# Raw blocks of the column-split W2 in tiles of 1024 columns, in a pool that the attention half shares

## The chip, the cores and the metric

The kernel runs on one core of a Trainium2 chip. The metric is the device time of one execution in microseconds (us). Of the kernel before there are three runs: 1780.76, 1771.97 and 1772.99 us, median 1772.99. A profiled execution was taken beside them. The core has TensorE (PE, with its weight loads as PEld), VectorE (DVE), ScalarE (ACT), GpSimd (POOL) and SyncE (SP), and 16 DMA engines.

## The reference

Two layers over 512 tokens of 1024 channels, in float32. Each layer:

```python
u = rms_norm(h, attn_norm[l])
proj = u @ w_in[l]                 # three mixers' q, k, v and the gates
a = differential_attention(...)    # 4 heads
r = bidirectional_retention(...)   # 4 heads
c = grouped_query_attention(...)   # 8 query heads
projected = einsum('bsnw,nwd->bsnd', [a, r, c], w_branch[l])
merged = sum(sigmoid(gates) * projected)
h = h + merged @ w_out[l]
m = square(relu(rms_norm(h, mlp_norm[l]) @ w_mlp_in[l]))   # 1024 -> 4096
h = h + m @ w_mlp_out[l]                                   # 4096 -> 1024 (W2)
```

## The kernel before

Every float32 operand of a matmul is held as two parts, hi and lo: ScalarE copies the operand to hi (a cast), VectorE subtracts hi from it to get lo, and TensorE adds three products (hi·hi, hi·lo, lo·hi). Weights come from memory in blocks of 128x1024 (512 KB) and are cut in this way just before use; `prefetch` does so two steps ahead.

A layer has two halves. In the attention half (`mix`) the projections and gates run woven with the heads (`ret_head`, `diff_head`, `gqa_head`). Each head ends in a pair of tiles hi and lo (`rTh`/`rTl`, `aTh`/`aTl`, `cTh`/`cTl`), which `proj_unit` multiplies by the branch weights, first those of the retention (merge 1), then the differential attention (merge 0), then the grouped attention (merge 2). In the MLP half, W1 runs in pairs of column blocks (`pair`, seven products of 128x256 matmuls each, PSUM tiles `x12`, `x674` and `x53`; each product is copied out by ScalarE to `pu` or `c0`). A pair takes two `stage` loads of 512 KB; the pool `stage` has two buffers. W2 is in four groups of 1024 rows. Groups 0 to 2 (`WIDE_GROUPS`) multiply by seven products of a two-by-two block scheme (`wide_product`), whose left operands are sums of the blocks A11, A12, A22 and A21 of W2. `cut_wide` loads the raw blocks, adds them in place (S1, S2, S4, S3) and cuts the sums; each raw block is held as two tiles of 128x512 out of the pool `g`, each loaded, added and cut by itself. The results of the seven products go to `sums` in memory: written by SyncE for group 0, added by a GpSimd DMA for groups 1 and 2. `gather` reads them back in tiles of 128x512 (`wp`), combines them on VectorE, turns them with TensorE and adds them to `h`, while group 3 runs as plain products.

Nearly all tiles of 128x512, of both halves, come from `g`, which has 51 buffers.

The order of the instructions is not that of the code: all operations are recorded and a planner (`order`) sets the order of each engine ahead of time. It steps through planned time; when an engine is free, it takes the first waiting operation in the recorded order whose inputs are ready and whose tiles have room in their pool (`fits`, where a tile may take a buffer only if those recorded earlier keep theirs). Its prices are `price`, `HOPS` and, for a load of SyncE, bytes / 360 ns and 2000 ns to land. What stands on an engine's list then runs in that order, so an instruction that waits holds back all that stands behind it. Every recorded matmul has line L455 in the profile and nearly every other instruction L461, so rows are told apart by tiles.

```python
            raw[x, k] = [self.g(x) for _ in range(2)]
            for i, t in enumerate(raw[x, k]):
                self.nc.sync.dma_start(out=t, in_=self.a["w"][at][:, i * 512:(i + 1) * 512])
```

Of the kernel before, what the change touches and what calls it, by code (L numbers as in the profile page):

```python
# [170 lines left out]
BUFS_G = 51  # L171
# [300 lines left out]
class Core:  # L472
    def __init__(self, ctx, tc, a):
# [13 lines left out]
        self.p_g = pool("g", BUFS_G)  # L487
        self.p_small = pool("small", 12)
# [26 lines left out]
    def g(self, name, dt=F32):  # L515
        return self.p_g.tile([128, 512], dt, tag="g", name=name)

# [69 lines left out]
    def cut_wide(self, q, op, k):  # L587
# [4 lines left out]
        def load(x):  # L592
            at = q + (int(x[1]) - 1) * 4 + (int(x[2]) - 1) * 2 + k
            raw[x, k] = [self.g(x) for _ in range(2)]
            for i, t in enumerate(raw[x, k]):
                self.nc.sync.dma_start(out=t, in_=self.a["w"][at][:, i * 512:(i + 1) * 512])

        def add(x, y):
            for t, o in zip(raw[x, k], raw[y, k]):
                self.nc.vector.tensor_tensor(out=t, in0=t, in1=o, op=ALU.add)  # L600
# [6 lines left out]
        hi, lo = self.parts(self.p_w, 1024)  # L607
        for i, t in enumerate(raw[x, k]):
            c = slice(i * 512, i * 512 + 512)
            self.nc.scalar.copy(out=hi[:, c], in_=t)  # L610
            self.nc.vector.tensor_tensor(out=lo[:, c], in0=t, in1=hi[:, c], op=ALU.subtract)
        return hi, lo
# [379 lines left out]
    def ret_head(self, h, st):  # L992
# [39 lines left out]
        hi, lo = self.g("rTh", F32R), self.g("rTl", F32R)  # L1032
# [62 lines left out]
    def diff_head(self, h, st):  # L1095
# [53 lines left out]
        hi, lo = self.g("aTh", F32R), self.g("aTl", F32R)  # L1149
# [9 lines left out]
    def gqa_head(self, j, kv, st):  # L1159
# [45 lines left out]
        if kv == 1:  # L1205
            hi, lo = self.g("cTh", F32R), self.g("cTl", F32R)
# [192 lines left out]
    def mlp(self, l, mT, h, mid, load, ready):  # L1399
# [14 lines left out]
        for what, g, i in mlp_order():  # L1414
# [14 lines left out]
            if g in WIDE_GROUPS:  # L1429
                if i == 0:  # L1430
                    rights = self.rights(m)
                    nxt = next(rights)
# [20 lines left out]
    def rights(self, m):  # L1453
# [5 lines left out]
        for n in WIDE_PRODUCTS:  # L1459
# [10 lines left out]
            for i in range(2):  # L1470
                hi, lo = self.g("xh", F32R), self.g("xl", F32R)
# [32 lines left out]
    def gather(self, h, mid, load, rp):  # L1504
# [3 lines left out]
        def back(n, s):  # L1508
            x = self.g("wp")
            nc.sync.dma_start(out=x, in_=self.sums[n, s])  # L1510
# [3 lines left out]
        u2, c = [None, None], [[None] * 4, [None] * 4]  # L1514
        for s in range(2):
            p1, p2, p6, p5, p3 = (back(n, s) for n in (1, 2, 6, 5, 3))
            tt(p2, p1, p2)
            tt(p6, p6, p1, ALU.subtract)
            tt(p5, p5, p6)
            tt(p3, p3, p5, ALU.subtract)  # L1520
            c[0][s], c[0][2 + s], u2[s] = p2, p3, (p6, p5)
        for half in range(2):
            if half:
                for s in range(2):
# [181 lines left out]
```

## Time and profile before

| what | value |
|---|---|
| runs | 1780.76, 1771.97, 1772.99 us; median 1772.99 us |
| profiled execution, its time | 1772.2 us |
| its span, first to last instruction | 1770.4 us |
| PE busy | 1744.6 us, 99% of the span |
| DVE busy | 1484.3 us, 84% |
| ACT busy | 1139.0 us, 64% |
| granted TensorE clock | 1.00 |
| loads of `stage` | 235, 512.0 KB each |
| loads of raw W2 blocks (`A`) | 96, 256.0 KB each |

How to read it: busy time of PE is modelled and matmuls overlap in it, so 99% does not say that TensorE never waits; what it waits for is seen in the waits of its weight loads (PEld). The list of waits names for each engine who waited for whom, in all and the longest. The timeline lists one engine's instructions with the idle time before each. Idle time of an engine that is not waited for costs nothing.

### The profile page before, as it was taken

Reading aid. Unit: us, or ns where it says so; the run is one execution under the profiler, and the core shown is the slowest. Engines: PE = TensorE matmul, PEld = TensorE weight load, DVE = VectorE, ACT = ScalarE, POOL = GpSimd, SP = SyncE. Lnnn points to the kernel's source line nnn. Section 1 sums busy time; section 2 is a strip of 40 time slices with the busy share of each in tenths; the row PEclk is TensorE's granted clock in tenths of the full one; section 3 lists DMA queues with packets and bytes.
Section 4 is the critical chain, followed back from the end, with each engine's and each line's share of the span. In section 5 each row is a group of like instructions: output and inputs, shape, how many; then the busy total and the mean of one; then the engine's idle time right before and its main releaser. Section 6 shows DMA issues by size and latency. Waiting matters only on the chain.

```text
span 1770.4 us, 27228 instructions
## 1 busy us (share of the span) xinstructions
PE 1744.6 (99%) x10136; PEld 1525.3 (86%) x10136; DVE 1484.3 (84%) x2438; ACT 1139.0 (64%) x2064; POOL 339.9 (19%) x350
## 2 busy tenths in 40 slices
PE   8999999999999999999999999999999999999999
PEld 6887888889988989988888778888899899989887
DVE  7866887899978999999866667978999789998994
ACT  5544666785556877777535456768855568777771
POOL 2334463001110001111013235700012100011110
PEclk9999999999999999999999999999999999999999
DMA  6311212112355354747622122111124542646482
GB/s 205 106 61 48 86 66 72 48 48 73 115 183 179 96 178 103 219 96 225 206 93 71 48 76 68 60 60 60 36 97 133 160 172 92 211 99 182 96 249 84
DMA packets 76741, 201.95 MB, mean 114 GB/s; under 512 B 8896, under 2 KB 9408, under 8 KB 76608
## 3 DMA queue, kind: packets, MB, share of 16 engines
q1 hardware_dynamic: 68544, 185.53, 32.0%
q0 software_dynamic: 8064, 14.68, 5.6%
q8 instruction: 79, 1.29, 0.3%
q14 instruction: 54, 0.44, 0.1%
HBM read 169.77 MB, written 30.41 MB: 113 GB/s over the span
## 4 chain that ended last, share of the span: by engine, by line
PE 73%; DVE 11%; DMA 6%; ACT 5%; issue 3%; POOL 2%; SPq 0%; ACTq 0%; DVEq 0%; POOLq 0%
PE x L455 19%; PE wide L455 7%; PE proj L455 6%; PE gate L455 6%; DMA stage<-in_w 6%; PE w L455 5%; PE wo L455 5%; PE c L455 4%; DVE w_lo L461 4%; PE wtr L457 2%; PE rg L455 2%; PE gsc L455 2%; PE gav L455 2%; PE dsc L455 2%; PE rq L455 1%
## 5 line engine op out<-in xcount | busy, mean ns | idle before, releaser
L461 ACT CAST w_hi<-stage 128x1024 fp32r<-128x1024 f32 (+1 forms) x235 | 226.8, 968 | 169.0 <-DMA stage<-in_w 95.4
L461 DVE TENSOR_TENSOR w_lo<-stage,w_hi 128x1024 fp32r<-128x1024 f32 (+1 forms) x235 | 282.0, 1202 | 35.1 <-ACT w_hi L461 31.9
L455 PE MATMUL x<-u,w_hi 128*128 128x256 f32 x1472 | 276.1, 283 | 0.0
L455 PEld LDWEIGHTS x<-u,w_hi 128*128 128x128 f32 x1472 | 233.5, 192 | 2.5
L455 PE MATMUL x<-u,w_lo 128*128 128x256 f32 x736 | 208.3, 283 | 0.0
L461 POOL DMA_DIRECT2D sums<-wp x56 | 49.1, 876 | 560.1 <-ACT xh L461 475.2
L455 PEld LDWEIGHTS x<-u,w_lo 128*128 128x128 f32 x736 | 141.1, 192 | 0.0
L455 PE MATMUL wide<-w_lo,xh 128*128 128x512 f32 x336 | 130.9, 390 | 0.0
L455 PE MATMUL wide<-w_hi,xl 128*128 128x512 f32 x336 | 130.8, 389 | 0.0
L455 PE MATMUL wide<-w_hi,xh 128*128 128x512 f32 x336 | 129.7, 390 | 0.0
L461 DVE TENSOR_TENSOR w_lo<-A,w_hi 128x512 fp32r<-128x512 f32 x168 | 112.3, 684 | 10.3 <-ACT w_hi L461 9.5
L455 PE MATMUL x<-t23h,w_hi 128*128 128x256 f32 x368 | 105.2, 287 | 3.3 <-ACT c L461 3.0
L461 ACT CAST w_hi<-A 128x512 fp32r<-128x512 f32 x168 | 102.2, 621 | 8.2 <-ACT w_hi L461 2.7
L455 PE MATMUL gate<-u,w_hi 128*128 128x512 f32 x320 | 106.4, 399 | 0.0
L461 ACT ACTIVATE c<-c 128x512 f32<-128x512 f32 x156 | 94.0, 628 | 19.0 <-DVE c L461 17.3
L455 PE MATMUL x<-t23h,w_lo 128*128 128x256 f32 x368 | 104.3, 283 | 0.3 <-DVE w_lo L461 0.2
L455 PE MATMUL x<-t23l,w_hi 128*128 128x256 f32 x368 | 104.1, 283 | 0.0
L455 PE MATMUL c<-w_hi,u 128*128 128x512 f32 x256 | 86.1, 394 | 0.0
L455 PEld LDWEIGHTS x<-t23h,w_hi 128*128 128x128 f32 x368 | 70.3, 191 | 5.9 <-ACT c L461 5.3
L461 POOL TENSOR_TENSOR gth<-gth,c 128x512 f32<-128x512 f32 x28 | 40.8, 1465 | 178.1 <-DVE c L461 178.0
L455 PEld LDWEIGHTS wide<-w_hi,xl 128*128 128x128 f32 x336 | 63.1, 188 | 13.1
L455 PEld LDWEIGHTS wide<-w_lo,xh 128*128 128x128 f32 x336 | 63.1, 188 | 12.5
(299 smaller groups left out, 5208.9 us busy)
## 6 DMA issues: line engine op xcount, KB each, us to landing
stage<-in_w SPq DMA_DIRECT2D x235, 512.0 KB, 3.6
A<-in_w SPq DMA_DIRECT2D x96, 256.0 KB, 4.6
sums<-wp POOLq DMA_DIRECT2D x56, 256.0 KB, 6.0
sums<-wp SPq DMA_DIRECT2D x28, 256.0 KB, 2.8
wp<-sums SPq DMA_DIRECT2D x28, 256.0 KB, 4.7
h<-in_x SPq DMA_DIRECT2D x16, 256.0 KB, 4.4
mid<-h SPq DMA_DIRECT2D x16, 256.0 KB, 2.1
h<-mid SPq DMA_DIRECT2D x16, 256.0 KB, 6.3
```

Of the source, the lines that this page charges most:

```text
L455: self.nc.tensor.matmul(k.pop("out"), **k)
L457: self.nc.tensor.transpose(k["out"], k["in_"], k["identity"])
L461: getattr(getattr(self.nc, o.engine), o.name)(**k)
```

## The change

Two pools take the place of one. `g` goes from 51 to 36 buffers of 128x512, and a new pool `b` has 8 buffers of 128x1024 (`big`), 52 buffers' worth of space together. In `b` lie

- the raw blocks of W2: one load of 512 KB for two of 256 KB, one addition of 128x1024 for two of 128x512, one cast and one subtraction for two of each (`part`);
- the hi and lo parts of `rT`, of `aT` and of the last two heads' pairs of `cT`, as the two halves of one tile (`big_parts`);
- the two last operands of the last wide group (`xb`, products 3 and 7);
- the tiles of `gather` (`wpb`): still two loads of 256 KB each, but one addition for both halves.

Count by engine: VectorE has 2292 instructions where it had 2438, ScalarE's casts and copies fall by 84, SyncE issues 428 DMAs for 476, TensorE and GpSimd have as many as before.

```diff
-BUFS_G = 51
+BUFS_G = 36
+BUFS_B = 8
...
+        self.p_b = pool("b", BUFS_B)
...
+    def big(self, name, dt=F32):
+        return self.p_b.tile([128, 1024], dt, tag="b", name=name)
+    def big_parts(self, name):
+        t = self.big(name, F32R)
+        return t[:, 0:512], t[:, 512:1024]
...
         def load(x):
             at = q + (int(x[1]) - 1) * 4 + (int(x[2]) - 1) * 2 + k
-            raw[x, k] = [self.g(x) for _ in range(2)]
-            for i, t in enumerate(raw[x, k]):
-                self.nc.sync.dma_start(out=t, in_=self.a["w"][at][:, i * 512:(i + 1) * 512])
+            raw[x, k] = self.big(x)
+            self.nc.sync.dma_start(out=raw[x, k], in_=self.a["w"][at])
         def add(x, y):
-            for t, o in zip(raw[x, k], raw[y, k]):
-                self.nc.vector.tensor_tensor(out=t, in0=t, in1=o, op=ALU.add)
+            self.nc.vector.tensor_tensor(out=raw[x, k], in0=raw[x, k], in1=raw[y, k], op=ALU.add)
...
-        hi, lo = self.parts(self.p_w, 1024)
-        for i, t in enumerate(raw[x, k]):
-            c = slice(i * 512, i * 512 + 512)
-            self.nc.scalar.copy(out=hi[:, c], in_=t)
-            self.nc.vector.tensor_tensor(out=lo[:, c], in0=t, in1=hi[:, c], op=ALU.subtract)
-        return hi, lo
+        return self.part(self.p_w, 1024, raw[x, k])
...
-        hi, lo = self.g("rTh", F32R), self.g("rTl", F32R)
+        hi, lo = self.big_parts("rT")
...
-        hi, lo = self.g("aTh", F32R), self.g("aTl", F32R)
+        hi, lo = self.big_parts("aT")
...
-            hi, lo = self.g("cTh", F32R), self.g("cTl", F32R)
+            hi, lo = self.big_parts("cTb") if j >= 2 else (self.g("cTh", F32R), self.g("cTl", F32R))
...
-                hi, lo = self.g("xh", F32R), self.g("xl", F32R)
+                hi, lo = self.big_parts("xb") if last and n in (3, 7) else (self.g("xh", F32R), self.g("xl", F32R))
...
-        def back(n, s):
-            x = self.g("wp")
-            nc.sync.dma_start(out=x, in_=self.sums[n, s])
+        def back(n):
+            x = self.big("wpb")
+            for s in range(2):
+                nc.sync.dma_start(out=x[:, s * 512:(s + 1) * 512], in_=self.sums[n, s])
             return x
...
-        for s in range(2):
-            p1, p2, p6, p5, p3 = (back(n, s) for n in (1, 2, 6, 5, 3))
-            tt(p2, p1, p2)
-            tt(p6, p6, p1, ALU.subtract)
-            tt(p5, p5, p6)
-            tt(p3, p3, p5, ALU.subtract)
-            c[0][s], c[0][2 + s], u2[s] = p2, p3, (p6, p5)
+        p1, p2, p6, p5, p3 = (back(n) for n in (1, 2, 6, 5, 3))
+        tt(p2, p1, p2)
+        tt(p6, p6, p1, ALU.subtract)
+        tt(p5, p5, p6)
+        tt(p3, p3, p5, ALU.subtract)
+        c = [both(p2, p3), both(p6, p5)]
```

The planner lays the whole program out anew. Up to the first gates and grouped-attention heads that lie side by side (about 350 us into each layer in the profile) the order on TensorE, VectorE, ScalarE and GpSimd is the same as before; in the merge it differs by some places, and in the MLP half TensorE's order is again nearly the same. Three places follow.

ScalarE in the first layer's attention, where a differential head's exponential `dE1` is written (`dwh` are turned softmax weights, `w_hi` a cut weight block; in brackets what each waits for, numbers tell tiles apart). Before:

```order
L461 CAST dwh_2406<-wtr_2349 128x512 [waits PE_49]
L461 ACTIVATE dE1_2413,dss_2376<-dsc_2367,mx_2392 128x512 [waits DVE_49]
L461 CAST w_hi_2423<-stage_2150 128x1024 [waits DMAHW4_49,PE_49]
L461 CAST w_hi_2438<-stage_2179 128x1024 [waits DMAHW5_49,PE_49]
L461 ACTIVATE dE1_2413<-dE1_2413,drc_2433 128x512 [waits DVE_49,Activation_49]
```

Now:

```order
L463 CAST dwh_2403<-wtr_2346 128x512 [waits PE_49]
L463 ACTIVATE dE1_2410,dss_2373<-dsc_2364,mx_2389 128x512 [waits DVE_49,Pool_49]
L463 CAST w_hi_2420<-stage_2148 128x1024 [waits DMAHW4_49,PE_49]
L463 CAST w_hi_2435<-stage_2177 128x1024 [waits DMAHW5_49,PE_49]
L463 ACTIVATE dE1_2410<-dE1_2410,drc_2430 128x512 [waits DVE_49,Activation_49]
```

The order is the same; the exponential `dE1` of the second row now waits for GpSimd too, since its buffer of `g` was one that a GpSimd instruction used.

ScalarE in the second layer, in the second wide group, where a pair of W1 is cut (`stage`, `sa`) while products are copied out (`c`, `pu`) and raw W2 blocks (`A`) are cut. Before:

```order
L461 CAST xh<-t_17281 128x512
L461 COPY c_17371<-x_17338 128x256
L461 CAST w_hi<-stage 128x512
L461 CAST w_hi<-A_16950 128x512
L461 COPY pu<-x_17342 128x256
L461 COPY c_17371<-x_17338 128x256
L461 CAST w_hi<-A_16852 128x512
L461 CAST xh<-c_16404 128x256
L461 CAST w_hi<-stage 128x1024
```

Now:

```order
L463 COPY c_18014<-x_17987 128x256
L463 COPY pu<-x_18007 128x256
L463 CAST w_hi<-stage 128x512
L463 COPY c_18014<-x_17987 128x256
L463 CAST w_hi<-A_17473 128x1024
L463 CAST xh<-t_17866 128x512
L463 CAST w_hi<-A_17493 128x1024
L463 CAST w_hi<-stage 128x1024
L463 COPY c_18014<-x_17968 128x256
```

Between the cast of the first `stage` block and the next copy to `c` there were a cast of `A` and a copy to `pu`; now that copy stands right behind the cast, the copy to `pu` ahead of it, and the blocks of W2 are cut whole and later.

SyncE in the second layer, from the last loads of the third wide group to the reads of `gather` (`stage` are weight blocks of 512 KB, `A` raw W2 blocks, `wp` and `wpb` the sums read back). Before:

```order
L461 DMA A_17847<-in_w 128x512
L461 DMA A_17855<-in_w 128x512
L461 DMA stage<-in_w 128x1024 x4
L461 DMA A_18185<-in_w 128x512
L461 DMA A_18194<-in_w 128x512
L461 DMA A_18217<-in_w 128x512
L461 DMA A_18229<-in_w 128x512
L461 DMA stage<-in_w 128x1024 x4
L461 DMA wp<-sums_101 128x512
L461 DMA wp<-sums_103 128x512
L461 DMA wp<-sums_107 128x512
```

Now:

```order
L463 DMA A_17493<-in_w 128x1024
L463 DMA A_17507<-in_w 128x1024
L463 DMA A_17528<-in_w 128x1024
L463 DMA stage<-in_w 128x1024 x8
L463 DMA wpb<-sums_104 128x512
L463 DMA wpb<-sums_106 128x512
L463 DMA wpb<-sums_105 128x512
L463 DMA wpb<-sums_110 128x512
L463 DMA wpb<-sums_107 128x512
```

The four late loads of `A` no longer stand between the loads of `stage`, and all eight raw blocks of the group stand ahead of eight loads of `stage`.

## Rows read from the trace of the kernel before

**Rows 1.** The page: its first line, part 1 (busy time of each engine, share of the span, instructions), one line of part 2 (the granted clock in 40 slices, tenths), and one of part 4 (the chain that ended last, by engine).

```profile
span 1770.4 us, 27228 instructions
...
PE 1744.6 (99%) x10136; PEld 1525.3 (86%) x10136; DVE 1484.3 (84%) x2438; ACT 1139.0 (64%) x2064; POOL 339.9 (19%) x350
...
PEclk9999999999999999999999999999999999999999
...
PE 73%; DVE 11%; DMA 6%; ACT 5%; issue 3%; POOL 2%; SPq 0%; ACTq 0%; DVEq 0%; POOLq 0%
```

**Rows 2.** The waits of TensorE's weight loads over the whole run (who waited for whom: us in total, times, longest): seven of the 23 rows, the first and the last among them.

```profile
PEld x L455 <- ACT c L461: 9.6, 17, 1.3
PEld rv L455 <- ACT w_hi L461: 7.1, 1, 7.1
PEld dsc L455 <- ACT dkh L461: 4.0, 6, 0.9
...
PEld qtr L457 <- POOL qk L461: 3.6, 4, 1.3
PEld rav L455 <- DVE sdl L461: 2.1, 1, 2.1
PEld gsc L455 <- ACT gE L461: 1.9, 4, 0.7
...
PEld rav L455 <- ACT sdh L461: 0.2, 1, 0.2
```

**Rows 3.** The same view for the stretch of the first layer's column-split products, 590 to 870 us.

```profile
PEld x L455 <- ACT c L461: 2.6, 5, 1.1
PEld x L455 <- DVE w_lo L461: 0.3, 1, 0.3
```

**Rows 4.** The same view from 1460 us to the end, the second layer's.

```profile
PEld x L455 <- ACT c L461: 5.8, 7, 1.3
...
PEld x L455 <- DVE w_lo L461: 0.4, 1, 0.4
```

**Rows 5.** The same view for 400 to 590 us: the merge of the first layer and the products behind it.

```profile
PEld x L455 <- ACT c L461: 0.6, 3, 0.3
```

**Rows 6.** ScalarE's instructions in order of time, 1568 to 1577 us (start us, us, engine, line, operation, out<-in; in brackets the idle time before it and what ended it).

```profile
1569.92 0.39 ACT L461 COPY c<-x 128x256 f32<-128x256 f32 x1
1573.06 0.62 ACT L461 CAST w_hi<-stage 128x512 fp32r<-128x512 f32 x1 [2.75 <-DMA stage<-in_w]
1573.58 0.61 ACT L461 CAST w_hi<-A 128x512 fp32r<-128x512 f32 x1
1574.10 0.36 ACT L461 COPY pu<-x 128x256 f32<-128x256 f32 x1
1574.37 0.37 ACT L461 COPY c<-x 128x256 f32<-128x256 f32 x1
```

**Rows 7.** TensorE's, in the same microseconds (the gap in brackets is the idle time of the modelled matmul).

```profile
1573.47 0.28 PE L455 MATMUL x<-u,w_lo 128*128 128x256 f32 x1
1574.79 0.39 PE L455 MATMUL x<-t4h,w_hi 128*128 128x256 f32 x1 [1.04 <-ACT c L461]
```

**Rows 8.** The DMA issues of SyncE ahead of them, 1560 to 1577 us.

```profile
1565.24 1.23 SPq L461 DMA_DIRECT2D stage<-in_w  x2
```

**Rows 9.** The view of the tile `stage`, 1440 to 1710 us: time from issue to landing (min, median, max), and then the same view for 100 to 300 us.

```profile
DMA to landing us min/median/max: 3.3/5.4/7.8
...
DMA to landing us min/median/max: 3.4/3.5/4.5
```

**Rows 10.** The waits of ScalarE, 1460 us to the end.

```profile
ACT w_hi L461 <- DMA stage<-in_w: 25.2, 12, 3.6
```

**Rows 11.** Groups by line, engine, operation and shape, 1460 us to the end (busy us, mean ns of one, idle time before them).

```profile
L461 DVE TENSOR_TENSOR w_lo<-A,w_hi 128x512 fp32r<-128x512 f32 x84 | 56.2, 684 | 6.2 <-ACT w_hi L461 5.8
L461 ACT CAST w_hi<-A 128x512 fp32r<-128x512 f32 x84 | 51.1, 621 | 3.8 <-ACT w_hi L461 1.8 <-PE wide L455 1.0 <-DVE A L461 0.8
...
L461 DVE TENSOR_TENSOR A<-A,A 128x512 f32<-128x512 f32 x48 | 31.7, 683 | 0.0
...
L461 DVE TENSOR_TENSOR w_lo<-sb,w_hi 128x1024 fp32r<-128x1024 f32 x13 | 15.8, 1219 | 0.4 <-ACT w_hi L461 0.4
...
L461 ACT CAST w_hi<-sb 128x1024 fp32r<-128x1024 f32 x13 | 13.7, 1054 | 0.8 <-DVE sb L461 0.3
...
L461 DVE TENSOR_TENSOR wp<-wp 128x512 f32<-128x512 f32 x14 | 9.2, 683 | 0.0
```

**Rows 12.** Busy time by stretch: the column-split products of the first and the second layer.

```profile
core 0: us, PE busy (x) PEld busy (x) DVE busy (x) ACT busy (x) POOL busy (x), PEclk, DMA share, GB/s
590.00:870.00 280.00, 278.33 (x1748) 251.67 (x1747) 263.23 (x460) 209.91 (x400) 24.61 (x28) 1.00 0.58 160
1460.00:1720.00 260.00, 255.44 (x1646) 232.51 (x1645) 238.91 (x428) 197.05 (x389) 24.46 (x28) 1.00 0.56 152
```

**Rows 13.** The DMA issues of the stretch 1440 to 1710 us (count, KB each, median us to landing).

```profile
stage<-in_w SPq DMA_DIRECT2D x28, 512.0 KB, 5.4
A<-in_w SPq DMA_DIRECT2D x36, 256.0 KB, 4.6
sums<-wp POOLq DMA_DIRECT2D x28, 256.0 KB, 6.4
```

**Rows 14.** In the first layer's attention: the GpSimd instructions from 232 us, then the ScalarE instructions from 241 us, then the same two for 264 and 274 us.

```profile
233.23 1.29 POOL L461 TENSOR_TENSOR gqx<-gqx,axy 128x512 f32<-128x512 f32 x1
...
241.53 0.70 ACT L461 ACTIVATE dE<-dsc,mx 128x512 f32<-128x512 f32 x1
...
267.15 0.46 POOL L461 TENSOR_TENSOR gk<-gkx,axy 128x128 f32<-128x128 f32 x1
...
274.46 0.70 ACT L461 ACTIVATE dE<-dsc,mx 128x512 f32<-128x512 f32 x1
```

More of the change, by code (lines that the diff above doesn't have):

```diff
@@ L1430, in mlp @@
                 if i == 0:
-                    rights = self.rights(m)
+                    rights = self.rights(m, g == WIDE_GROUPS[-1])
                     nxt = next(rights)
@@ L1451, in mlp, with rights @@
             ready(i, h[i])
-    def rights(self, m):
+    def rights(self, m, last):
         nc = self.nc
@@ L1506, in gather @@
         nc = self.nc
-        def back(n, s):
-            x = self.g("wp")
-            nc.sync.dma_start(out=x, in_=self.sums[n, s])
+        def back(n):
+            x = self.big("wpb")
+            for s in range(2):
+                nc.sync.dma_start(out=x[:, s * 512:(s + 1) * 512], in_=self.sums[n, s])
             return x
         tt = lambda out, x, y, op=ALU.add: nc.vector.tensor_tensor(out=out, in0=x, in1=y, op=op)
-        u2, c = [None, None], [[None] * 4, [None] * 4]
-        for s in range(2):
-            p1, p2, p6, p5, p3 = (back(n, s) for n in (1, 2, 6, 5, 3))
-            tt(p2, p1, p2)
-            tt(p6, p6, p1, ALU.subtract)
-            tt(p5, p5, p6)
-            tt(p3, p3, p5, ALU.subtract)
-            c[0][s], c[0][2 + s], u2[s] = p2, p3, (p6, p5)
+        both = lambda *xs: [x[:, s * 512:(s + 1) * 512] for x in xs for s in range(2)]
+        p1, p2, p6, p5, p3 = (back(n) for n in (1, 2, 6, 5, 3))
[4 more added lines that the diff above has]
+        c = [both(p2, p3), both(p6, p5)]
         for half in range(2):
             if half:
-                for s in range(2):
-                    p7, p4 = back(7, s), back(4, s)
-                    p6, p5 = u2[s]
-                    tt(p5, p5, p7, ALU.subtract)
-                    tt(p6, p6, p7, ALU.subtract)
-                    tt(p6, p6, p4)
-                    c[1][s], c[1][2 + s] = p6, p5
+                p7, p4 = back(7), back(4)
+                tt(p5, p5, p7, ALU.subtract)
+                tt(p6, p6, p7, ALU.subtract)
+                tt(p6, p6, p4)
             for t, x in enumerate(c[half]):
```

## Prediction

> **What bounds the kernel now.** I began with the page. TensorE is busy for 99% of the span, at the full granted clock in every slice, and holds 73% of the chain that ended last [rows 1]. So the span is TensorE's own work, and an edit that adds or removes no matmul can only move what TensorE waits. Its busy time is modelled and hides short waits, so I went on to what its weight loads wait for [rows 2]: 23 rows that add up to some 43 us. That is the ceiling of any gain here, 2.4% of the span. Most of it has nothing to do with W2: 7.1 us are the first weights at the start, and the rows with `dsc`, `qtr`, `rav` and `gsc` are the heads of the attention half. What lies near the change is the first row, W1's products `x` that wait for ScalarE's copies to `c`: 9.6 us in 17 waits.
>
> Taken by stretch, 2.6 us of them in 5 waits, with 0.3 us for `w_lo`, lie in the first layer's wide groups [rows 3], 5.8 us in 7 waits, with 0.4 us for `w_lo`, in the second's [rows 4], and little in between, such as 0.6 us around the first merge [rows 5]. So 9.1 us are within the change's reach.
>
> Then I followed one of them back, the one near 1574 us. TensorE finishes a product at 1573.47 us and takes up the next at 1574.79 us, after a copy to `c` [rows 7]. ScalarE had been idle for 2.75 us, since the cast of a `stage` block stands ahead of that copy on its list and the block had not landed; then the cast, a cast of `A`, a copy to `pu` and only then `c` at 1574.37 us [rows 6]. The load was issued at 1565.24 us, with the other block of its pair [rows 8]. Loads of `stage` here need 3.3 to 7.8 us to land, 5.4 in the median, against 3.5 us in the quiet attention half [rows 9]; the planner allowed for some 3.5 us. In this layer ScalarE waits 25.2 us for such loads in 12 waits [rows 10], of which 5.8 reach TensorE. So the path is: load of `stage` late, ScalarE held, bank not emptied, TensorE waits.
>
> **The change part by part.** *Splits of W2.* Six wide groups with seven operands in two blocks are 84 splits. On VectorE each took two subtractions of 684 ns and now takes one of the size of `w_lo<-sb`, 1219 ns: 149 ns less, 12.5 us in all. On ScalarE two casts of 621 ns become one of 1054 ns: 188 ns less, 15.8 us in all [rows 11]. *Sums of W2.* 48 additions of 1219 ns take the place of 96 of 683 ns [rows 11]: 7.1 us less, if the addition costs what the subtraction of that size does. *Gather.* 14 operations for 28 of 683 ns [rows 11]: 2.1 us less. Together VectorE loses 21.7 us and ScalarE 15.8 us. None of it is on the path as work: VectorE is busy for 263.2 of 280 us and 238.9 of 260 us in the two stretches, ScalarE for 209.9 and 197.1 us, under TensorE's 278.3 and 255.4 us [rows 12]. By itself it is worth 0.
>
> *When `stage` is free.* It has an indirect worth. A load of `stage` is issued when VectorE has finished with the buffer, and VectorE is 92 to 94% busy there. It saves about 10.9 us a layer, over 12 pairs of W1 that are cut in a layer's wide stretch (the 12 waits of rows 10 are of this kind): 0.9 us a pair. If all of that lead reaches the load, each of the 12 waits of TensorE, 8.4 us together and 0.7 us in the mean, shrinks by up to 0.9 us, and hardly any is left; if the DMA queue and not VectorE sets the landing, none shrinks. Two things of the order speak for the first: at the place shown the copy to `c` stands right behind the cast, without a cast of `A` and a copy to `pu` between (0.5 and 0.3 us by the steps of rows 6); and in the last wide group the late loads of `A` no longer stand between loads of `stage`. One speaks against it: GpSimd's adding DMAs, 28 with a median of 6.4 us to landing [rows 13], run beside them as before. I take 0.4 us a wait, between the ends, nearer the middle than the full lead: 12 x 0.4 = 4.8 us less. Bounds: 0 and 9.1 us.
>
> *Fewer, larger loads of W2.* 48 loads of 512 KB for 96 of 256 KB. In this stretch an `A` of 256 KB needs 4.6 us and a `stage` of 512 KB 5.4 us [rows 13]; none of the waits above names `A`, so this is 0, save for what it clears for `stage`, which is counted above. The Trainium skill, DMA: Bandwidth & Descriptors, section "Anatomy of one DMA", gives a fixed 2 us for each transfer besides its bytes; by that, two loads would cost 2 us more than one of the same bytes, and the queue ahead of `stage` would empty so far that every wait of the stretch goes, 1763.1 us. The minimum of 3.3 us for 512 KB agrees with it, the median of 5.4 us does not: there the other transfers count.
>
> *The pool `g`, 51 to 36.* The order of the attention half is unchanged up to the merge, so what can come there is a wait for a buffer. The tightest new waits that I found are two exponentials of the differential heads that wait for GpSimd. In the trace the first starts at 241.53 us and its releaser, from 233.23 us on for 1.29 us, had ended 7.0 us before; the second at 274.46 us, and its releaser, from 267.15 us for 0.46 us, 6.9 us before [rows 14]. So these cost 0; the cover is that lead, and beyond it each microsecond would be ScalarE's.
>
> *The merge.* The order there changes by some places. Its waits are 0.6 us in 3 [rows 5]; I allow the change 0.3 us more, between 0.6 us less and 4 us more, the latter if three of its `stage` casts wait as the longest of rows 4, 1.3 us each.
>
> *The sum.* The profiled execution took 1772.2 us: the span of 1770.4 us and 1.8 us around it. 1772.2 - 4.8 + 0.3 = 1767.7 us. The median of the runs lies 0.8 us higher, so I put 1768 us, 0.3% less than the median of 1773.0 us. A measurement of this kernel can tell about 0.5% from no change, 8.9 us.
>
> **The rivals.**
> (a) *All waits of the stretch go.* VectorE's lead reaches the loads in full: 1772.2 - 9.1 = 1763.1 us, 1763.9 us on the median. For it: 0.9 us against a mean of 0.7 us. Against it: the long waits, 1.3 us at most [rows 4], are above the lead, and the adding DMAs stay.
> (b) *It is hidden anyway.* The engines relieved were not waited for, the landing of `stage` is set by the queue: the waits stay as they are, 1772 to 1773 us. For it: an idle VectorE shortens no transfer, and the planner puts the cast where it believes the load to have landed, as before.
> (c) *Slower: the loads of `A` in one lump.* All eight blocks of a group stand in a row ahead of `stage`, 4 MB at once, where twelve halves and four late ones stood before. A load of `stage` behind them would land late; it decides from some 6.5 us after the issue, which in rows 6 to 8 is where TensorE began to wait. With four such pairs a layer, eight in all, and 2 to 3 us each, 16 to 24 us more: 1788 to 1796 us. Against it: each load of `A` waits for its own buffer of `b`, so they are spread by VectorE's work.
> (d) *Slower: too few buffers in `g`.* An evacuation waits for a tile, and TensorE for the evacuation, head by head. At the longest wait of `dsc` now, 0.9 us [rows 2], for each of the 32 heads of two layers: 29 us more, 1801 us. It decides where a new wait's lead of 6.9 us is used up; rows 14 speak against it. The Trainium skill, Perfetto Trace Analysis, section "Optimization Strategy", says that the same gap repeating on the engine that should be saturated can mean too little SBUF for the next tile, which is what (d) would look like; the trace of before has such small gaps in the heads already, with 51 buffers, behind casts and reductions and not behind freed tiles.
>
> **How the numbers follow.** Forecast 0.55, (a) 0.17, (b) 0.17, (c) 0.06, (d) 0.05. Faster by over 0.5% means under 1764.1 us: most of (a) and a little of the forecast, 0.17. Slower by over 0.5%: (c) and (d), 0.11. Within: 0.72. The forecast's own range is 1765 to 1772 us. The range reaches down to (a), 1763 us, and up over (b) to the merge's bound on top of it, 1773 + 4 = 1777 us; it leaves out (c), (d) and a little below.
>
> **What would show it.** VectorE's busy time down by some 22 us and ScalarE's by some 16 us; in the waits of the weight loads `x <- ACT c` at about 4 to 5 us instead of 9.6 us, with the rows of the attention half as they were; `ACT w_hi <- DMA stage` less than 25 us in the second layer's stretch. For (b) that row and `x <- ACT c` would stand as they do now; for (c) the landing of `stage` would rise above 5.4 us; for (d) GpSimd or VectorE would appear as releaser of ScalarE in the heads. I am wrong if the attention half, which I take as fixed, moves by more than 2 us, or if the reordered merge brings waits that none of its rows shows now.

## The result, and the profile after

The changed kernel takes **1790.9 us** in the median of 6 runs (1786.4 to 1797.0), the kernel before 1773.0 us (1770.3 to 1780.8, 6 runs). The ratio is 1.0101, 95% interval 1.0084 to 1.0117: slower by 1%, 18 us, and outside the range of 1763 to 1777 us. The profiled execution is the slowest of the six, 1797.0 us, so what its profile adds up to is some 6 us more than the median's loss. Of E8 below one run, 2459.9 us long at a mean granted clock of 0.65, is left out as a slow state.

The page of the changed kernel: its first line, part 1, and three rows of part 6 (DMA issues: count, KB each, median us to landing).

```profile
span 1795.2 us, 26933 instructions
...
PE 1754.1 (98%) x10136; PEld 1532.2 (85%) x10136; DVE 1474.1 (82%) x2292; ACT 1130.6 (63%) x1980; POOL 341.6 (19%) x350
...
stage<-in_w SPq DMA_DIRECT2D x235, 512.0 KB, 3.6
A<-in_w SPq DMA_DIRECT2D x48, 512.0 KB, 4.9
sums<-wp POOLq DMA_DIRECT2D x56, 256.0 KB, 6.3
```

Against [rows 1] the span is 24.8 us longer. TensorE executes the same 10136 matmuls, but they keep it busy 9.5 us longer (1754.1 for 1744.6 us); the other 15.3 us are new idle time. VectorE has lost 10.2 us and ScalarE 8.4 us of busy time, half of what was reckoned. The waits of the weight loads (PEld), whole run:

```profile
PEld x L457 <- ACT c L463: 24.5, 18, 3.4
PEld rv L457 <- ACT w_hi L463: 7.1, 1, 7.1
PEld dsc L457 <- ACT dkh L463: 4.6, 5, 2.0
...
PEld gsc L457 <- ACT gE L463: 3.3, 6, 0.7
```

Beside [rows 2] one row has moved far: `x <- ACT c`, from 9.6 to 24.5 us, with nearly as many waits (18 for 17) and a longest of 3.4 us for 1.3. Its rise, 14.9 us, is nearly as much as the new idle time. The same view by stretch: the first merge, the first layer's wide groups, the second merge, the second layer's wide groups.

```profile
PEld x L457 <- ACT c L463: 1.6, 2, 1.3
...
PEld x L457 <- ACT c L463: 8.6, 5, 3.4
...
PEld x L457 <- ACT c L463: 3.9, 4, 1.4
...
PEld x L457 <- ACT c L463: 10.4, 7, 2.9
```

Against [rows 3 to 5]: 6.0 us more in the first wide stretch, 4.6 us more in the second, 1.0 and 3.3 us more in the merges (the second merge of before has 0.6 us, as the first). The longest wait is near 745 us. ScalarE's instructions in order of time from 737 us on, and then TensorE's (start, duration; in brackets the idle time before):

```profile
737.60 0.59 ACT L463 COPY wp<-wide 128x512 f32<-128x512 f32 x1 [0.72 <-PE wide L457]
741.53 1.05 ACT L463 CAST w_hi<-stage 128x1024 fp32r<-128x1024 f32 x1 [3.35 <-DMA stage<-in_w]
742.48 0.36 ACT L463 COPY pu<-x 128x256 f32<-128x256 f32 x1
744.14 0.62 ACT L463 CAST w_hi<-stage 128x512 fp32r<-128x512 f32 x1 [1.29 <-DMA stage<-in_w]
744.66 0.36 ACT L463 COPY c<-x 128x256 f32<-128x256 f32 x1
```

```profile
741.59 0.28 PE L457 MATMUL x<-u,w_lo 128*128 128x256 f32 x1
745.08 0.58 PE L457 MATMUL x<-t23h,w_hi 128*128 128x256 f32 x1 [3.21 <-ACT c L463]
745.46 0.41 PE L457 MATMUL x<-t23l,w_hi 128*128 128x256 f32 x1
745.67 0.41 PE L457 MATMUL x<-t23h,w_lo 128*128 128x256 f32 x1
```

The picture is that of [rows 6, 7], only larger. TensorE's last matmul starts at 741.59 us and the next at 745.08 us; it waited for the copy to `c`, which stands on ScalarE's list behind the casts of the two `stage` blocks, and ScalarE sat 3.35 and 1.29 us until those had landed. In the kernel before, the same copy stands ahead of the cast of the second block:

```profile
740.46 0.38 ACT L461 COPY c<-x 128x256 f32<-128x256 f32 x1
740.72 0.63 ACT L461 CAST w_hi<-stage 128x512 fp32r<-128x512 f32 x1
```

So in the changed kernel the copy waits for a second landing too. That order alone does not make the wait: E5 below keeps it and has none here. SyncE issued them at 732.89 and 733.50 us, as early as in the kernel before (733.03 and 733.67 us). They landed late. The view of the tile `stage`, 731 to 740 us, first before, then after (the two loads of the one pair: min, median, max):

```profile
DMA to landing us min/median/max: 6.2/6.6/7.0
```

```profile
DMA to landing us min/median/max: 8.6/9.6/10.6
```

One thing more is in the matmuls behind the wait: the last two rows start 0.21 us apart, where matmuls of this shape at the full clock start 0.12 us apart. Busy time by stretch of 4 us, and the granted clock (the number behind POOL's):

```profile
core 0: us, PE busy (x) PEld busy (x) DVE busy (x) ACT busy (x) POOL busy (x), PEclk, DMA share, GB/s
738.00:742.00 4.00, 3.87 (x33) 3.66 (x31) 0.00 (x0) 0.65 (x2) 1.02 (x2) 1.00 1.07 294
742.00:746.00 4.00, 0.92 (x4) 0.92 (x5) 1.79 (x3) 2.71 (x6) 0.00 (x0) 0.76 0.64 127
746.00:750.00 4.00, 4.00 (x21) 4.00 (x21) 4.00 (x6) 2.51 (x4) 0.00 (x0) 0.50 0.25 62
750.00:754.00 4.00, 4.00 (x32) 4.00 (x32) 3.92 (x5) 1.44 (x2) 0.00 (x0) 0.89 0.49 200
754.00:758.00 4.00, 4.00 (x35) 4.00 (x35) 3.09 (x5) 2.26 (x6) 0.00 (x0) 1.00 0.00 0
```

From the last microsecond of the idle stretch on, the granted clock is 0.50, the 1.2 GHz level, for some 7 us, and then full again. The clock falls in the same way behind the waits of 2.3 us near 784, 2.0 us near 1145 and 2.9 us near 1642 us, and nowhere ahead of the last matmul in the profile of the kernel before, whose longest wait after the start is 2.1 us. By the granted clock, these four stretches make the matmuls some 10 us longer, about the 9.5 us of busy time. They also spread the runs: the six runs of the changed kernel have mean clocks of 0.994 to 0.999, the slowest run the lowest.

### The profile page after: what moved, and what is told of

The parts are those of the page before. It is cut to its first block, busy times and chain, and to the rows that moved or that the text cites. A ratio compares the mean times of both kernels' runs of the same rounds, so it can differ in the third digit from the quotient of the medians.

```text
span 1795.2 us, 26933 instructions
## 1 busy us (share of the span) xinstructions
PE 1754.1 (98%) x10136; PEld 1532.2 (85%) x10136; DVE 1474.1 (82%) x2292; ACT 1130.6 (63%) x1980; POOL 341.6 (19%) x350
## 3 DMA queue, kind: packets, MB, share of 16 engines
q8 instruction: 79, 1.29, 0.3%
## 4 chain that ended last, share of the span: by engine, by line
PE 72%; DVE 9%; DMA 7%; ACT 5%; POOL 3%; issue 2%; SPq 0%; DVEq 0%; ACTq 0%; POOLq 0%
PE x L457 18%; PE wide L457 8%; DMA stage<-in_w 6%; PE gate L457 6%; PE proj L457 5%; PE w L457 5%; PE wo L457 5%; PE c L457 4%; DVE w_lo L463 3%; PE wtr L459 2%; PE rg L457 2%; PE rq L457 2%; PE dsc L457 2%; PE gsc L457 2%; PE rk L457 2%
## 5 line engine op out<-in xcount | busy, mean ns | idle before, releaser
L457 PE MATMUL wide<-w_hi,xh 128*128 128x512 f32 x304 | 118.6, 390 | 0.0
L457 PE MATMUL wide<-w_lo,xh 128*128 128x512 f32 x304 | 118.5, 390 | 0.0
L457 PE MATMUL wide<-w_hi,xl 128*128 128x512 f32 x304 | 118.3, 389 | 0.0
L463 DVE TENSOR_TENSOR w_lo<-A,w_hi 128x1024 fp32r<-128x1024 f32 x84 | 102.1, 1221 | 15.2 <-ACT w_hi L463 15.1
L463 ACT CAST w_hi<-A 128x1024 fp32r<-128x1024 f32 x84 | 87.9, 1052 | 18.2 <-PE x L457 10.1
L463 POOL TENSOR_TENSOR gth<-gth,c 128x512 f32<-128x512 f32 x28 | 44.5, 1602 | 182.6 <-DVE c L463 182.6
L457 PEld LDWEIGHTS x<-t23h,w_lo 128*128 128x128 f32 x368 | 71.5, 195 | 0.5 <-DVE w_lo L463 0.4
L457 PEld LDWEIGHTS x<-t23l,w_hi 128*128 128x128 f32 x368 | 71.6, 195 | 0.2
```

What stands on the lines that cost most here:

```text
L457: self.nc.tensor.matmul(k.pop("out"), **k)
L463: getattr(getattr(self.nc, o.engine), o.name)(**k)
```

## Experiments

Theory L: the eight loads of W2 in a lump ahead of a `stage` pair make the pair land late, and the path of [rows 6 to 8] does the rest. The rivals are in the expectations. Waits are in us, `x <- ACT c`, of the one profiled execution, which in E2, E3 and E6 is 7.6, 13.0 and 3.3 us faster than the median and in E11 7.5 us slower: first wide stretch (590 to 890 us), second (from 1480 us), both merges (400 to 590 and 1290 to 1480 us). "Landing" is the pair near 733 us.

| Kernel | Median us | Ratio, 95% interval | Wide 1, wide 2, merges | TensorE busy | Landing |
|---|---|---|---|---|---|
| before | 1773.0 | 1 | 2.6, 5.8, 1.2 | 1744.6 | 6.2, 7.0 |
| changed | 1790.9 | 1.0101, 1.0084 to 1.0117 | 8.6, 10.4, 5.5 | 1754.1 | 8.6, 10.6 |
| E1 A21 later (planner) | 1771.9 | 0.9998, 0.9986 to 1.0010 | 4.1, 0.4, 3.5 | 1743.5 | 8.2, 10.1 |
| E2 two DMAs a block | 1794.1 | 1.0116, 1.0092 to 1.0141 | 8.3, 7.8, 3.5 | 1748.4 | 9.6, 11.1 |
| E3 sums and splits in halves | 1807.4 | 1.0186, 1.0147 to 1.0225 | 9.1, 8.7, 4.8 | 1752.8 | 9.7, 11.3 |
| E4 old gather | 1787.4 | 1.0078, 1.0054 to 1.0103 | 9.8, 8.4, 4.3 | 1747.9 | 9.5, 11.5 |
| E5 A21 later (SyncE only) | 1782.1 | 1.0044, 1.0024 to 1.0064 | 6.4, 5.3, 4.5 | 1748.6 | 6.2, 7.0 |
| E6 E1, A21 sooner (SyncE only) | 1780.0 | 1.0039, 1.0025 to 1.0053 | 7.2, 1.6, 4.3 | 1745.7 | 7.7, 9.7 |
| E7 E1 and old gather | 1771.0 | 0.9993, 0.9983 to 1.0003 | 2.7, 1.3, 4.4 | 1743.6 | 7.1, 9.5 |
| E8 E1, casts planned later | 1796.6 | 1.0148, 1.0123 to 1.0172 | 0, 0, 0 | 1754.8 | none there |
| E9 E5 and `stage` freed sooner | 1779.5 | 1.0037, 1.0023 to 1.0050 | 5.0, 5.1, 5.0 | 1744.3 | 7.3, 8.4 |
| E10 E9 and old gather | 1772.3 | 1.0002, 0.9990 to 1.0015 | 1.7, 1.9, 4.9 | 1743.9 | 7.3, 7.7 |
| E11 E7 and `stage` freed sooner | 1772.5 | 0.9997, 0.9985 to 1.0009 | 3.4, 0, 5.6 | 1748.4 | 5.2, 7.6 |
| E12 before, `stage` freed sooner | 1772.1 | 1.0002, 0.9989 to 1.0014 | 1.6, 0.5, 2.8 | 1743.3 | 5.6, 6.8 |
| E13 changed, sums not added | 1768.0 | 0.9971, 0.9957 to 0.9985 | 1.6, 0, 5.4 | 1744.1 | 7.0, 7.7 |
| E14 before, sums not added | 1765.2 | 0.9945, 0.9925 to 0.9964 | 1.5, 0.9, 0.8 | 1742.3 | 4.4, 5.1 |
| E15 before, 44 buffers in `g` | 1845.4 | 1.0398, 1.0371 to 1.0425 | 0.7, 1.8, 3.3 | 1772.5 | 3.6 |

**E1, the loads of A21 held back in the plan.** In `cut_pair` the index of the pair's last load is kept; in `cut_wide` the load of A21 depends on it:

```diff
+        self.pair_at = len(self.nc.ops) - 1
...
             self.nc.sync.dma_start(out=raw[x, k], in_=self.a["w"][at])
+            if x == "A21":
+                self.nc.ops[-1].deps.add(self.pair_at)
```

> The two loads of A21 may not be issued before the stage pair that stands ahead of them in program order, so 3 MB instead of 4 MB of W2 stand ahead of that pair. Theory L (the lump of eight 512 KB loads makes the stage pair behind it land 8.6 and 10.6 us after its issue, so ScalarE and then TensorE wait, and the clock falls afterwards): the waits of 3.4 and 2.9 us near 745 and 1641 us go or fall under 1.5 us, that pair lands in about 6 to 7 us as before the change, and the median is 1779 to 1784 us (of 1790.9). Rival S (512 KB transfers as such share the queue worse) and rival W (1024-wide instructions hold ScalarE's and VectorE's lists longer): within 2 us of 1790.9. Rival G (what is lost comes from the gather or from the smaller pool g): the same, 1789 to 1793.

The whole loss is gone, 19 us and not the 7 to 12 that L asked for. The second layer waits 0.4 us instead of 10.4 us, and the clock falls nowhere. But the pair of the first layer still lands 8.2 and 10.1 us after its issue, with six loads ahead of it and not eight, and TensorE waits 2.6 us for it. So the number of loads does not set the landing by itself, and what does in E1 is not shown; E1 did not win in the way foreseen alone. The planner had also put ScalarE's, VectorE's and SyncE's lists behind it in another order. E5 and E6 take the two apart.

**E2, the size of a transfer; E3, the length of an instruction.** E2 fetches each block by two DMAs:

```diff
-            self.nc.sync.dma_start(out=raw[x, k], in_=self.a["w"][at])
+            for i in range(2):
+                c = slice(i * 512, i * 512 + 512)
+                self.nc.sync.dma_start(out=raw[x, k][:, c], in_=self.a["w"][at][:, c])
```

> Each 1024-wide block of W2 is fetched by two DMAs of 256 KB into its halves; nothing else is changed. Theory L: the same bytes stand ahead of the stage pair, so 1788 to 1794 us, with the pair's landing still at 8 us or more. Rival S: the landing falls to about 6 to 7 us and the median to 1775 to 1781 us.

E3 adds and splits the wide tiles in halves:

```diff
-            self.nc.vector.tensor_tensor(out=raw[x, k], in0=raw[x, k], in1=raw[y, k], op=ALU.add)
+            for i in range(2):
+                c = slice(i * 512, i * 512 + 512)
+                self.nc.vector.tensor_tensor(out=raw[x, k][:, c], in0=raw[x, k][:, c], in1=raw[y, k][:, c], op=ALU.add)
...
-        return self.part(self.p_w, 1024, raw[x, k])
+        hi, lo = self.parts(self.p_w, 1024)
+        for i in range(2):
+            c = slice(i * 512, i * 512 + 512)
+            self.split(raw[x, k][:, c], hi[:, c], lo[:, c])
+        return hi, lo
```

> Sums and splits of W2 are done in 512-wide halves as before the change, on the 1024-wide tiles. Theory L: the loads are where they were, so no gain: 1788 to 1796 us (VectorE busy about 20 us more, ScalarE 16 us more). Rival W: 1774 to 1780 us, since long instructions no longer stand ahead of the copies to c.

Neither size nor length makes the loss: with half loads it is the same, with half instructions it is larger by some 16 us. E3's plan was laid anew, so how much of the 16 us is the instructions themselves is not shown. The Trainium skill (DMA: Bandwidth & Descriptors, "Anatomy of one DMA") gives a fixed 2 us for each transfer of GpSimd's path, mostly completion latency. A cost of that kind for each of SyncE's loads does not show here: E2's interval overlaps that of the changed kernel.

**E4, the old gather.** `gather` is that of the kernel before: 28 operations of 512 columns, tiles of pool `g`, the first halves of all five sums and then the second.

> Only the gather of the sums is as before the change (28 operations of 512 columns, tiles of pool g, halves one after the other). Theory L: the two waits near 745 and 1641 us stay, and at most the 1.5 to 1.8 us each near 832 and 1727 us go: 1786 to 1791 us. Rival G: 1776 to 1782 us.

3.5 us less, with intervals that overlap; E10 decides it.

**E5 and E6, the place of two loads and nothing else.** The finished order of the changed kernel (E5) or of E1 (E6) is kept; only SyncE's two loads of A21 are moved in it, behind the next `stage` pair or ahead of it:

```diff
+    def moved(self, order):
+        wait, seen = [], 0
+        for i in order:
...
+            if name == "A21":
+                wait.append(i)
...
+            if name == "stage" and wait:
+                seen += 1
+                if seen == 2:
+                    yield from wait
...
-        for i in self.order():
+        for i in self.moved(self.order()):
```

> The changed kernel with every engine's list as it is, but on SyncE's the two loads of A21 stand behind the stage pair that they stood ahead of. Theory L1 (the place of those two loads alone makes the loss): the pair at 733 us lands in 6 to 8 us, TensorE's waits near 745 and 1641 us fall to 1.5 us or less, no fall of the clock there, 1774 to 1781 us. Rival P (E1's gain came from the rest of the plan that it changed on ScalarE and VectorE, above all from earlier stage loads behind that pair): 1785 to 1791 us.

> E1's kernel with every other engine's list as it is, but on SyncE's the two loads of A21 stand ahead of the stage pair again. L1: the pair lands in 9 us or more, TensorE waits 3 us or more behind it in both layers, the clock falls, 1780 to 1790 us. Rival P: 1771 to 1776 us.

In either plan the place of these two loads is worth about the same, 8.8 us (1790.9 to 1782.1) and 8.0 us (1771.9 to 1780.0), with intervals apart. In E5 the pair near 733 us lands after 6.2 and 7.0 us, exactly as before the change, and the wait behind it is gone. Both theories are half right: the rest of the plan is worth another 10 to 11 us (1782.1 to 1771.9 and 1790.9 to 1780.0).

In its profiled run E6's loss does not stand where L1 foresaw it. Near 749 us TensorE waits 2.2 us, in the second layer 0.7 us at most, and the clock does not fall there. The longest wait, 3.0 us, and the only fall of the clock ahead of the kernel's end stand near 666 us, in the second wide group. There the pair is issued at 656.8 us, right behind A21 and 1.5 us later than in E1, and ScalarE waits for it. Its landing (655 to 662 us; in E1 4.3 and 4.7 us) and ScalarE's row:

```profile
DMA to landing us min/median/max: 7.0/7.5/7.9
```

```profile
663.85 1.04 ACT L479 CAST w_hi<-stage 128x1024 fp32r<-128x1024 f32 x1 [5.19 <-DMA stage<-in_w]
```

GpSimd's queue moves nothing from 640 to 670 us, so here the two loads did this without adding DMAs.

Most of what E5 still waits stands near 778 and 827 us, and near 1664 and 1712 us. The first of these in the changed kernel itself (near 784 us there), on VectorE (765.9 to 776 us):

```profile
766.25 1.22 DVE L463 TENSOR_TENSOR w_lo<-stage,w_hi 128x1024 fp32r<-128x1024 f32 x1
...
771.09 0.68 DVE L463 TENSOR_TENSOR sb<-stage,sa 128x512 f32<-128x512 f32 x1
...
775.31 0.69 DVE L463 TENSOR_TENSOR w_lo<-stage,w_hi 128x512 fp32r<-128x512 f32 x1
```

The pair's first `stage` buffer is free when `sb<-stage,sa` is done, the second when the half block is split, at 775.31 us; ten short instructions stand between the first block's split and the one, and four short and two wide ones between that and the other. SyncE issues the pair at 771.85 and 776.02 us. In the kernel before, the two instructions stand at 766.76 and 765.83 us, and the loads at 766.57 and 767.47 us.

**E7, E1 with the old gather; E8, casts planned later.** E7 puts E4's edit on E1:

> E1 and E4 together: A21's loads held back and the gather as it was before the change. Theory L with E4's 3.5 us as a part of its own: the wait of 1.4 us near 825 us goes, 1768 to 1771 us. If E4's gain was only the wait that E1 removes as well: 1771 to 1773 us.

E8 changes one number in E1's planner:

```diff
-    LATENCY = {"sync": 2000.0}
+    LATENCY = {"sync": 4000.0}
```

> E1, and the planner counts 4.0 us instead of 2.0 us from the end of a SyncE issue to its landing, so that casts of stage are placed later and stage loads earlier. If the landing of stage is what the remaining waits of x for c come from (8.1 us in 8 waits in E1's profile), they fall to 2 to 4 us and the time to 1766 to 1769 us. If placing the casts later only moves the wait to the weights themselves: 1771 to 1776 us, with new waits for w_hi or w_lo.

E7 is level with the kernel before (the interval reaches 1.0003). E8 fails in a way that neither branch had: no wait for `c` is left, but the weights come late instead, 3.8 us each time in the first products of W1 behind `wo`, and the heads wait longer. Its first row of waits:

```profile
PEld x L457 <- ACT w_hi L463: 8.7, 4, 3.8
```

**E9 and E10, the other two places.** E9 is E5, and in the finished order the two instructions of VectorE are moved up to the split of the pair's first block:

```diff
+    def sooner(self, order):
+        for p in self.pairs.values():
+            at = {x: n for n, x in enumerate(order)}
+            for i in p["move"]:
+                to = 1 + max(at[x] for x in (p["a"], *self.ops[i].deps))
+                if to < at[i]:
+                    order.insert(to, order.pop(at[i]))
```

> E5, and on VectorE the two instructions that free the two stage buffers of a pair (the second sum sb<-stage,sa and the split of the last half block) stand right behind the split of the pair's first block, instead of some ten short subtractions later. Theory B (the second wait of a layer, near 778 and 1664 us in E5, is a stage load that SyncE issued too late because VectorE's list freed its buffer late): both waits of 2.3 us and the falls of the clock behind them go, 1774 to 1778 us (of 1782.1). Rival Q (the landing of 7 us beside the adding DMAs makes that wait whenever the load is issued): 1780 to 1784 us.

E10 adds the old gather:

> E9 and the gather of before the change. If the loss has three places a layer (A21's loads, the late stage load, the gather) that add up, all three are undone here with the wide tiles kept: 1771 to 1775 us, level with the kernel before (1772 to 1773). If they are one chain in which the first sets off the others: like E9.

In E9 the waits near 778 and 1664 us are gone, and so is every fall of the clock; the time, 1779.5 us, lies between the two forecasts and is 2.6 us less than E5's, which the intervals don't tell apart. In E10 the old gather takes off 7.2 us more, with intervals apart, and the kernel with wide tiles is level with the kernel before. The three steps from 1790.9 us make 8.8, 2.6 and 7.2 us. E10's waits by stretch, in the order of the four rows above:

```profile
PEld x L487 <- ACT c L493: 2.4, 2, 1.8
...
PEld x L487 <- ACT c L493: 1.7, 3, 0.8
...
PEld x L487 <- ACT c L493: 2.5, 2, 1.7
...
PEld x L487 <- ACT c L493: 1.9, 2, 1.1
```

**E11 and E12, a faster version?** E9's order of VectorE on E7 and on the kernel before:

> E7 with E9's order on VectorE. If stage loads that are issued 3 to 7 us sooner take away what E7 still waits in the wide stretches (2.7 and 1.3 us), 1767 to 1770 us, faster than the kernel before by 0.15 to 0.3%. If E7's remaining wait near 745 us is the landing behind W2's loads, whatever VectorE does: 1770 to 1772 us.

> The kernel before with E9's order on VectorE alone, no change of W2's tiles. If the late freeing of stage also makes a part of its 9.6 us of waits for c, 1766 to 1770 us. If the kernel before has its stage loads early enough where it matters: 1771 to 1775 us.

Neither is. E12 halves its waits for `c` (9.6 to 4.8 us) and takes the same time: 1.7 us of waits for `pu` and 1.1 us for `t23l` are new, and the rest lies within the interval. No version here beats the kernel before.

**E13 and E14, the adding DMAs.** GpSimd's DMAs of the products write `sums` and don't add; all lists stay as they are.

```diff
-                nc.gpsimd.dma_start(out=self.sums[n, s], in_=y, accum_op=ALU.add)
+                nc.gpsimd.dma_start(out=self.sums[n, s], in_=y)
```

> The changed kernel; GpSimd's DMAs of the wide products write the sums and do not add to them (the addition of the three groups is left out). All lists as they are. Theory L2 (the lump is late because it shares the queues with adding DMAs, which hold them about twice as long per byte): the pair near 733 us lands in 5 to 7 us, the waits near 745 and 1641 us fall under 1.5 us, 1770 to 1778 us. Rival (4 MB ahead of the pair are enough): landing stays at 8 us or more, 1786 to 1794 us.

> The kernel before with the same left out. L2: its waits in the wide stretches (2.6 and 5.8 us) shrink too, since they come from the same queue: 1765 to 1769 us. Rival: 1770 to 1773 us.

The changed kernel falls by 22.9 us, to 1768.0 us, the kernel before by 7.5 us, to 1765.2 us. So at this pair 4 MB ahead of it are not enough for the loss; they make it beside adding DMAs (near 666 us in E6 a pair was late without them). Without additions the change costs 2.8 us, with intervals that overlap. The landing falls less than L2 expected, to 7.0 and 7.7 us, and the time more, but the long waits are gone (1.6 us in the first wide stretch, none in the second) and the clock with them. DMA traffic from 690 to 860 us, first the changed kernel, then E13 (packets, MB, share of 16 engines; then the issues):

```profile
q1 hardware_dynamic: 7334, 20.87, 35.8%
q0 software_dynamic: 3752, 6.82, 25.1%
...
stage<-in_w SPq DMA_DIRECT2D x19, 512.0 KB, 5.9
sums<-wp POOLq DMA_DIRECT2D x26, 256.0 KB, 6.3
```

```profile
q1 hardware_dynamic: 7920, 22.48, 39.5%
q0 software_dynamic: 2080, 6.82, 10.8%
...
stage<-in_w SPq DMA_DIRECT2D x21, 512.0 KB, 4.1
sums<-wp POOLq DMA_DIRECT2D x26, 256.0 KB, 3.4
```

GpSimd's queue moves the same 6.82 MB, and with additions it holds the engines for 25.1% of the stretch, without for 10.8%: 2.3 times as long for a byte. In the changed kernel itself the second wide group agrees: there the products are still written and not added, the same eight loads stand ahead of the pair, and it lands 4.9 and 5.8 us after its issue (654 us).

**E15, fewer buffers.** `BUFS_G = 44` in the kernel before, nothing else.

> The kernel before with 44 buffers in pool g instead of 51, nothing else. If fewer buffers of 512 columns make the merge and the heads wait: the waits of x for c at 400 to 590 and 1290 to 1480 us rise from 0.6 to 2 us or more each, and the time to 1776 to 1782 us. If the pool's size is not what moved the merge: 1771 to 1775 us.

Much worse than either branch, 72 us. The waits of the merges for `c` rise only to 1.6 and 1.7 us; the first rows are others:

```profile
PEld gsc L455 <- ACT gE L461: 18.6, 19, 5.0
PEld x L455 <- ACT pu L461: 17.4, 12, 4.0
PEld dsc L455 <- ACT dE L461: 9.5, 13, 2.1
PEld wide L455 <- DVE xl L461: 8.3, 4, 3.4
```

The heads wait up to 5.0 us for `gE`, W1's products 17.4 us for `pu` and the wide products 8.3 us for `xl`: the planner's order is another one throughout. Whether the split into 36 and 8 is what costs the changed kernel its merges is not shown by this, since here W2's own blocks lie in `g` too.

## Why the prediction was wrong

**The step that failed** is "Fewer, larger loads of W2 ... so this is 0", with the reason that "none of the waits above names `A`". No wait names `A` after the change either. What the loads cost is laid on the pair behind them: it was issued as early as before and landed 2.4 to 3.6 us later. The size of the loads has no part in it (E2); their place on SyncE's list has (E5, E6: 8.8 and 8.0 us). At this pair it takes the adding DMAs with them (E13), which the prediction names as something that "speaks against" a gain, and not as what shares the DMA engines with the lump. The rest of the loss goes with the gather (7.2 us, below) and, within the noise, with a buffer freed late (2.6 us, E9).

**Rival (c)** was this mechanism, with all eight blocks of a group in a row, a landing past 6.5 us as the point of decision, and 1788 to 1796 us as its time. It got 0.06. The reason against it, that the loads of `A` "are spread by VectorE's work", is true and did not help: eight loads went out over 15.1 us, from 715.44 us on, and the longest landing among them was 8.4 us. That its time was met is in part luck: it counted eight late pairs of 2 to 3 us, and the profile has one long wait behind the lump in each layer (3.4 and 2.9 us), beside the other places and the clock. The trace of before held the warning: the longest landing of [rows 9], 7.8 us, is that of the pair that already stood behind three of the four MB, issued at 1612.52 us.

**What can move the span.** "An edit that adds or removes no matmul can only move what TensorE waits" is refuted: TensorE was busy 9.5 us longer with the same matmuls, since its clock fell behind four waits. The ceiling of the gain stood; for a loss there is no such ceiling.

**VectorE's and ScalarE's work.** 21.7 and 15.8 us were forecast, 10.2 and 8.4 us came. The durations of the rows overlap. VectorE before the change, 727.5 to 736.5 us:

```profile
728.18 1.28 DVE L461 TENSOR_TENSOR w_lo<-A,w_hi 128x512 fp32r<-128x512 f32 x2
729.38 0.68 DVE L461 TENSOR_TENSOR sb<-stage 128x512 f32<-128x512 f32 x1
...
734.20 1.21 DVE L461 TENSOR_TENSOR w_lo<-sa,w_hi 128x1024 fp32r<-128x1024 f32 x1
735.33 1.22 DVE L461 TENSOR_TENSOR w_lo<-sb,w_hi 128x1024 fp32r<-128x1024 f32 x1
736.47 0.41 DVE L461 TENSOR_TENSOR xl<-c,xh 128x256 fp32r<-128x256 f32 x1
```

Two splits of 512 columns take 1.28 us together, each lasting 0.68 us; the next starts 1.20 us after the first, 0.60 us each. The wide ones start 1.13 and 1.14 us apart and last 1.22 us. So a pair of halves gives back 0.06 us and not 0.149 us; 146 of them are some 9 us. The lead of 0.9 us a pair was half of that, too. (The sum's 1767.7 us and the 0.8 us of the median make 1768.5 us and not 1768; nothing hangs on it.)

**When `stage` is free.** The sum took 4.8 us off the wide stretches' waits of 9.1 us. In the change itself they rose. With the three places mended (E10) the waits for `c` are 3.6 us for 8.4 us. But E10 also moves VectorE's instructions, and the same move in the kernel before, with narrow tiles, leaves 2.1 us (E12). So that `stage` was free earlier by the shorter work is not shown, and fewer such waits did not by themselves shorten the kernel: E12 is no faster. Of the two things of the order that spoke for a gain, the first held at the place shown and was the other way round near 745 us, where the copy to `c` fell behind a second block.

**The merge.** 0.3 us was forecast, at most 4 us. The two merges wait 4.3 us more for `c` in the changed kernel, 3.7 us more in E10: at the upper bound and a little past it, by waits that the rows of before do not have, which the prediction names as a sign of being wrong. This takes back most of E10's 4.8 us in the wide stretches. In the changed kernel's wait near 444 us the copy to `c` stands behind the cast of `sa` on ScalarE's list (443.23 and 442.28 us); before, it stood ahead of it (441.08 and 442.32 us). VectorE's last addition into `sa` starts at the same time in both, 441.57 and 441.61 us. What in the change reorders ScalarE there is not settled.

**The pool `g`, rival (d).** The rows of the attention half move by 1.4 us at most (`gsc <- ACT gE`, 1.9 to 3.3 us), but the 0 did not hold in the profiled run: the wait of 2.0 us near 1145 us and the slow matmuls behind it, some 3 us by the granted clock, lie in that half. A wait of this size is in E11 and E12 too and not in E1, E9, E10 or E13, so that the smaller pool makes it is not shown. E15 shows that rival (d) has a price far above its 29 us, from a smaller pool than this change leaves.

**The gather** was counted as 2.1 us less on VectorE and nothing else. Its loads are a second lump: eight of 256 KB stand ahead of the pair near 824 us in the changed kernel, seven of them issued from 817.00 to 820.70 us, and the pair lands after 7.1 and 9.0 us. In the kernel before the eight are spread from 802.74 to 812.06 us, and the pair behind them lands after 5.9 and 7.7 us. The old gather in the new pools (E10) has none of its loads ahead of the pair, which lands after 6.0 and 6.2 us; it is better than before, not only undone. That is 7.2 us (E10 against E9). E10 changes the gather's additions and tiles along with its loads, so the loads' share of this is argued from the landings and not measured by itself.

## What to carry to other kernels

Before a change gives loads more room, look at which loads will move ahead of which on their queue, and at what else runs on the engines of the DMA just then: a planner that takes the first instruction that fits can let the new room pull early loads ahead of the late, urgent one. The wait was booked here on the urgent load, by name, and not on the two whose place caused it. Look also at where on an engine's list the instruction that the bounding engine waits for now stands. A wait of two or three microseconds on the bounding engine can cost more in its clock besides (here 9.5 us beside 15.3 us of idle time).

## What the runs showed of the hardware

- An adding DMA of GpSimd's queue held the 16 engines 2.3 times as long for a byte as one that writes (25.1% for 10.8% of 170 us, 6.82 MB each). The kernel before was 7.5 us faster without additions (E14).
- TensorE's granted clock fell to 0.50 behind waits of 2.0, 2.3, 2.9 and 3.4 us in the changed kernel, for up to 7 us, and did not fall behind a wait of 2.6 us in E1 and in E5 (near 745 and 827 us) or of 2.1 us in the kernel before. What else decides it stays open.
- Consecutive instructions of VectorE overlapped by some 0.08 us, so that 512 columns cost 0.60 us in a row and not the 0.68 us of the profile.
- Near 1140 us, in the second layer's heads, a single load of `stage` with little beside it took 5.9 us instead of some 3.5 us in the changed kernel, 6.4 us in E11 and 5.6 us in E12, and TensorE waited 2.0, 2.5 and 1.7 us behind it. In these three runs it was issued 1.1 us behind its neighbour, as in the kernel before and E14, where it took 4.6 us. In E1 to E7, E9, E10 and E13 it took 3.5 to 4.0 us, issued some 2.2 us behind. That this is the cause was not tried.
